# One broadcast multiply in place of eight scalings per row, and final waits in the order of the stores, in a grouped softmax

## The chip, the cores and the metric

One core of one Trainium2 chip. The metric is device time in microseconds (us), median of several executions; lower is better. A program on a single core gives "fast" runs here that lie within a few tenths of a microsecond, with a rare one 3 to 14 us above.

## The reference

```python
B, N, D, G = 4, 4096, 4352, 8          # x: float32
x_g = x.reshape(B, N, G, D // G)
x_g = x_g - x_g.max(axis=-1, keepdims=True)
exp = np.exp(x_g)
out = exp / exp.sum(axis=-1, keepdims=True)
```

A softmax over eight groups of 544 elements in each of 16384 rows. 285.2 MB are read and 285.2 MB written; the arithmetic is small.

## The kernel before

The 16384 rows are 64 tiles of 128 partitions by 2 rows (4.456 MB each). Six buffers in SBUF go round. SyncE issues the loads and, ahead of each after the sixth, waits for the store that frees the buffer. ScalarE issues the stores; the store of tile j-2 waits until VectorE has *seen* tile j land, so loads and stores alternate. VectorE takes the maxima of the next row before it scales the present one.

```python
P, R, NT, G, LAG = 128, 2, 6, 8, 2          # partitions, rows per tile, buffers, groups, lag of stores
def vector_max(n):
    s = n % S
    if s % R == 0:
        take(nc.vector, landed[s // R], 16)
        nc.vector.sem_inc(seen, 1)
    nc.vector.reduce_max(out=mx[:, s, :], in_=row(s), axis=X, negate=True).then_inc(max_done, 1)

def vector_scale(n):
    s = n % S
    take(nc.vector, exp_done)
    nc.vector.reciprocal(out=rs[:, s, :], in_=sm[:, s, :]).then_inc(rec_done, 1)
    take(nc.vector, rec_done)
    xr = row(s)
    for g in range(G):
        i = nc.vector.tensor_scalar_mul(
            out=xr[:, g, :], in0=xr[:, g, :], scalar1=rs[:, s, g:g + 1])
    i.then_inc(scaled, 1)
# ... scalar_exp: eight activations with accumulated sums; store: waits for `scaled`, R rows ...
for t in range(nt):
    b = t % NT
    if t >= NT:
        nc.sync.wait_ge(stored[b], 16 * (t // NT))
    nc.sync.dma_start(out=bufs[b][:, :], in_=xt[t]).then_inc(landed[b], 16)
for b in range(NT):
    nc.sync.wait_ge(stored[b], 16 * ((nt - b + NT - 1) // NT))
# ... VectorE: rows in the order vector_max(n + 1), vector_scale(n) ...
```

## Time and profile before

| | before |
|---|---|
| time, median of 3 | 1330.06 us (1329.78 to 1330.08) |
| span of the profiled execution | 1328.5 us |
| busy: VectorE, ScalarE | 78%, 58% |
| transfers | 570.4 MB, 429 GB/s over the span |
| last load landed, as seen by VectorE | 1280.54 us |
| last store issued | 1303.55 us |

How to read it: an engine that is busy 78% on average could still set the time in some stage, so ask in each stage who waits for whom. From 165 us on VectorE waits for a landing in each tile, and the DMA row is full; the transfers set the time.

### The profile page before, as it was taken

The numbers are of one execution on the slowest core, as the hardware profiler recorded it, in microseconds if no ns is written. First come the engines' busy times: TensorE is split into PE (matmuls) and PEld (weight loads), VectorE is DVE, ScalarE is ACT, GpSimd is POOL, SyncE is SP. The second block draws the span as 40 slices with busy tenths as digits, with TensorE's granted clock in tenths as the row PEclk, the third lists the DMA queues.
The fourth block names the chain that finished last, engine by engine and source line by source line (L and its number), as shares of the span: only waits on it lengthen the run. The fifth ranks groups of instructions, "written<-read, shape, count | busy, mean of one in ns | idle before, by whom it ended". The sixth has DMA issues, their size and how long they took to land. (4 is left out here: it accounts for less than half of the span.)

```text
span 1328.5 us, 4328 instructions
## 1 busy us (share of the span) xinstructions
DVE 1041.7 (78%) x1280; ACT 764.5 (58%) x2049; POOL 0.2 (0%) x4
## 2 busy tenths in 40 slices
DVE  5899987887877878778787787877878778787781
ACT  3677755655556556565565655655556555565551
POOL 0000000000000000000000000000000000000000
DMA  9999999999999999999999999999999999999997
GB/s 403 418 436 435 434 433 429 432 435 436 435 433 428 432 435 436 435 434 430 429 436 435 435 434 433 426 436 436 434 434 433 427 435 436 435 434 433 427 433 328
DMA packets 18439, 570.49 MB, mean 429 GB/s; under 512 B 2048, under 2 KB 2048, under 8 KB 2048
## 3 DMA queue, kind: packets, MB, share of 16 engines
q1 hardware_dynamic: 9216, 285.22, 49.8%
q10 hardware_dynamic: 9216, 285.22, 49.7%
q14 instruction: 7, 0.06, 0.0%
HBM read 285.21 MB, written 285.21 MB: 429 GB/s over the span
## 5 line engine op out<-in xcount | busy, mean ns | idle before, releaser
L88 ACT ACTIVATE xt<-xt,mx 128x544 f32<-128x544 f32 x1024 | 751.3, 735 | 534.1 <-ACTq L59 534.1
L70 DVE TENSOR_REDUCE mx<-xt 128x8 f32<-128x4352 f32 x128 | 599.2, 4682 | 238.3 <-DVEq L59 235.3
L79 DVE TENSOR_SCALAR xt<-xt,rs 128x544 f32<-128x544 f32 x1024 | 434.2, 498 | 19.2
L88 ACT ACTIVATION_READ_ACCUMULATOR xt<-xt,mx 128x1 f32 x1024 | 192.0, 187 | 0.0
L75 DVE RECIPROCAL rs<-sm 128x8 f32<-128x8 f32 x128 | 24.8, 193 | 4.2 <-DVEq L59 4.2
L120 ACT ACT_TABLE_LOAD x1 | 1.3, 1283 | 0.9 <-SPq L47 0.9
L156 POOL MEMSET const-bfloat16-1.0<- 128x1 bf16 x1 | 0.1, 103 | 0.0
L156 POOL MEMSET const-uint8-127<- 128x1 uint8 x1 | 0.1, 102 | 0.0
L156 POOL MEMSET const-float32-0.0<- 128x1 f32 x1 | 0.1, 100 | 0.2 <-issue 0.2
L156 POOL MEMSET const-float32-1.0<- 128x1 f32 x1 | 0.1, 99 | 0.0
## 6 DMA issues: line engine op xcount, KB each, us to landing
xt<-in_x_dram SPq DMA_DIRECT2D x64, 4352.0 KB, 30.5
out_dram<-xt ACTq DMA_DIRECT2D x64, 4352.0 KB, 51.3
```

What stands on the lines that cost most here:

```text
L70: nc.vector.reduce_max(out=mx[:, s, :], in_=row(s), axis=X, negate=True).then_inc(max_done, 1)
L75: nc.vector.reciprocal(out=rs[:, s, :], in_=sm[:, s, :]).then_inc(rec_done, 1)
L79: i = nc.vector.tensor_scalar_mul(out=xr[:, g, :], in0=xr[:, g, :], scalar1=rs[:, s, g:g + 1])
L88: i = nc.scalar.activation(out=xr[:, g, :], in_=xr[:, g, :], func=Exp, bias=mx[:, s, g:g + 1], scale=1.0, accum_out=sm[:, s, g:g + 1],)
L120: nc.scalar.preload_act_table(Exp)
L156: nc = _bacc.Bacc("TRN2", target_bir_lowering=False, num_devices=1)
```

## The change

The intent is to spend fewer VectorE instructions per row: one multiply of 4352 elements, whose second input repeats each group's reciprocal 544 times (a step of 0), in place of eight scalings of 544 elements. The final waits are put in the order in which the stores were issued. The "two rings" of its description, loads on one queue and stores on another, are in both kernels.

```diff
-        for g in range(G):
-            i = nc.vector.tensor_scalar_mul(
-                out=xr[:, g, :], in0=xr[:, g, :], scalar1=rs[:, s, g:g + 1])
-        i.then_inc(scaled, 1)
+        nc.vector.tensor_tensor(
+            out=xr,
+            in0=xr,
+            in1=rs[:, s, :].unsqueeze(2).to_broadcast([P, G, Dg]),
+            op=mybir.AluOpType.mult,
+        ).then_inc(scaled, 1)
...
-    for b in range(NT):
-        nc.sync.wait_ge(stored[b], 16 * ((nt - b + NT - 1) // NT))
+    for t in range(nt - NT, nt):
+        nc.sync.wait_ge(stored[t % NT], 16 * (t // NT + 1))
```

## The prediction

> **What bounds the kernel now.** I read the page first: the busy shares, the slices of DMA, the groups by line. Then the engines' waits, VectorE's timeline in the middle and at both ends, and the DMA share in short windows at the end.
>
> ```profile
> span 1328.5 us, 4328 instructions
> DVE 1041.7 (78%) x1280; ACT 764.5 (58%) x2049; POOL 0.2 (0%) x4
> DMA  9999999999999999999999999999999999999997
> HBM read 285.21 MB, written 285.21 MB: 429 GB/s over the span
> L70 DVE TENSOR_REDUCE mx<-xt 128x8 f32<-128x4352 f32 x128 | 599.2, 4682 | 238.3 <-DVEq L59 235.3
> L79 DVE TENSOR_SCALAR xt<-xt,rs 128x544 f32<-128x544 f32 x1024 | 434.2, 498 | 19.2
> L75 DVE RECIPROCAL rs<-sm 128x8 f32<-128x8 f32 x128 | 24.8, 193 | 4.2 <-DVEq L59 4.2
> ```
>
> No compute engine is full: VectorE (DVE) is busy 78% of the span, ScalarE 58%. The DMA row is full from the first slice to the last but one, at 429 GB/s. Each byte is moved once in and once out, 570.4 MB, so 128 tile moves of 4.456 MB. VectorE stands 235.3 us before its max reductions, and the releaser is a wait of its own queue: a tile that has yet to land. The timeline of VectorE in the middle shows one tile of two rows:
>
> ```profile
> 1239.18 4.68 DVE L70 TENSOR_REDUCE mx<-xt 128x8 f32<-128x4352 f32 x1 [4.09 <-DVEq L59]
> 1243.79 0.19 DVE L75 RECIPROCAL rs<-sm 128x8 f32<-128x8 f32 x1
> 1244.13 3.39 DVE L79 TENSOR_SCALAR xt<-xt,rs 128x544 f32<-128x544 f32 x8
> 1247.44 4.68 DVE L70 TENSOR_REDUCE mx<-xt 128x8 f32<-128x4352 f32 x1
> 1252.03 0.19 DVE L75 RECIPROCAL rs<-sm 128x8 f32<-128x8 f32 x1
> 1252.37 3.39 DVE L79 TENSOR_SCALAR xt<-xt,rs 128x544 f32<-128x544 f32 x8
> 1259.88 4.69 DVE L70 TENSOR_REDUCE mx<-xt 128x8 f32<-128x4352 f32 x1 [4.11 <-DVEq L59]
> ```
>
> A tile takes 1259.88 - 1239.18 = 20.70 us. VectorE works about 16.6 us of it and waits 4.1 us, and this wait returns every 20.7 us from 165 us on. At 20.7 us for two moves of 4.456 MB the DMA does 431 GB/s. So the steady stage is set by the transfers; VectorE has 4.1 us per tile, 2.05 us per row, to spare. The end, in windows (width, then busy of DVE, ACT, POOL, clock, DMA share, GB/s):
>
> ```profile
> 1280.60:1303.60 23.00, 19.82 (x29) 11.92 (x32) 0.00 (x0) 1.00 1.01 434
> 1303.60:1320.00 16.40, 0.00 (x0) 0.00 (x0) 0.00 (x0) 1.00 0.96 416
> 1320.00:1326.00 6.00, 0.00 (x0) 0.00 (x0) 0.00 (x0) 1.00 0.08 35
> ```
>
> The last store is issued at 1303.55, but a tile takes only 4.456 MB / 434 GB/s = 10.3 us and the DMA is full until about 1320. So 1320 - 1303.55 - 10.3 = about 6 us of older stores were still queued before it. Even the last store did not find idle transfer engines.
>
> **What the Trainium skill says.** "VectorE: DVE Perf Modes", section "The perf-mode tier table", gives fp32 tensor_scalar two elements per cycle and fp32 tensor_tensor and tensor_reduce one. The trace agrees for the kernel before: eight scalings of 544 take 3.39 us, fewer than 4352 / 0.96 GHz = 4.53 us, and the reduction takes 4.68 us. The same page, section "The TRN2 errata", gives (N+151)/0.96 GHz for an fp32 tensor_tensor: an estimate of 4503 / 0.96 = 4690 ns here, close to the 4682 ns that the one-per-cycle reduction over the same 4352 elements is measured at. No tensor_tensor is in this trace, so that part is not yet shown. "DMA: Bandwidth & Descriptors", section "Where 436 GB/s comes from", gives a ceiling of 435.2 GB/s at the SBUF ports. 429 over the span and 434 near the end agree: the floor is 570.4 MB / 435.2 = 1311 us, and the rest of the span is the first 2 us, the tail, and less than 1% of loss. The same section names some 358 GB/s for HBM as the bound; this trace shows more, and the measurement decides.
>
> **The change, part by part.** (1) It removes 1024 scalings of 544 elements; eight take 3.39 us, 3.31 us from their start to the next reduction's. The 498 ns mean counts overlap, so I don't multiply it by eight. (2) It adds 128 multiplies of 4352 elements at one element per cycle. I take 4.69 us each, 4.61 us to the next start (as between the reduction at 1239.18 and the reciprocal at 1243.79). So the change makes VectorE slower by 4.61 - 3.31 = 1.30 us per row, although it has 896 fewer instructions. VectorE's busy time becomes 599.2 + 24.8 + 128 x 4.69 = 1224 us, 92% of the span. A tile takes it 16.6 + 2.6 = 19.2 us, still under 20.7: the wait for a landing shrinks from 4.1 to about 1.5 us. Steady cost on the path: 0.
>
> (3) The start. Until about 165 us VectorE, not the DMA, is behind: it works without waiting for a landing and stores go out every 16.5 us. The first loads keep the DMA busy anyhow: six tiles x 10.3 us lasts to about 63 us. Store 0 is issued at 48.61 after two rows' scalings in the chain, so about 2.6 us later now. The next should be issued between 63 and 71 us, and later ones every 19.1 us. Store 0 and the last load share the DMA until about 73 us, so store 1 arrives just in time; from there a store every 19.1 us is faster than the 20.7 us that a load and a store take, and the DMA's queue only grows. Catching up takes far longer than before, up to some 500 us, since only 1.5 us is gained per tile. That is hidden, but the queue is thin from 60 to 100 us. I allow 0 to 3 us, most likely 0.5.
>
> (4) The end. From the last landing (1280.54) VectorE has three scalings to do. The last row's chain is: reduction of the last row after one slower scaling (+1.3), exponentials, then its own scaling (+1.3). So the last store is issued at 1303.55 + 2.6 = 1306.2. About 6 us were queued before it, so about 3.4 us still are. On average this is hidden; if some engines run dry early, up to 2.6 us show. I count 0.3.
>
> (5) The final waits. Loads go out on one queue and stores on another in both kernels; only the order of the six final waits changes. The wait for buffer 3 (the last store) is followed by two that are already met, at some 28 ns each in the trace: 0.06 us less. Nothing.
>
> Sum: 1330.06 + 0.5 + 0.3 - 0.06 = 1330.8 us.
>
> **The rivals.** (a) VectorE becomes the bound. It does if a row takes more than 20.7 / 2 = 10.35 us, thus if the multiply takes over 3.31 + 2.05 = 5.36 us to the next start. Against it: the reduction reads the same 4352 elements in 4.68 us. For it: two inputs, one of them a broadcast with step 0 inside, of which I have no measured line. At two cycles per element it would be about 9.1 us, a row 14 us, the whole 128 x 14 = about 1800 us. I give this 2%. A fixed cost of 0.7 us more per instruction would be needed for even the first loss. (b) The delays of the two ends show in full: 2.6 at the end and 3 at the start, 1335.7 us. For it: the queue is thin at the start, and at the end only 3.4 us of backlog is left. Against it: the DMA share near both points shows no hole, and it needs every store to miss. (c) Fewer and longer instructions speed things up: VectorE's sequencer is done with a row after one instruction instead of eight, so it signals a landing earlier in the catching-up stage, and the loop's first pass has less to fetch (3.05 us of idle at 56.38 now). It would help only where VectorE is late, in the first 165 us, and there the DMA is already full: no gain, at most 1 us.
>
> **Range and chances.** The time is set by 570 MB at the ceiling in both kernels, and three runs before lie within 0.3 us. So the range is the two ends: 1328.8 (small luck in the order of transfers) to 1334.5 (most of the delays of 3 and 2.6 us exposed). Two per cent is 26.6 us; only rival (a) gets there. Faster 0.01, same 0.95, slower 0.04.
>
> **What would show it right or wrong.** Right: line 79 or so has 128 TENSOR_TENSOR of about 4690 ns; VectorE at about 1224 us and 92%; waits before reductions fall from 235 us to under 80 us (fewer than 40 tiles x 1.5 us, plus the first 14); 20.7 us from landing to landing in the middle; about 429 GB/s; the last store issued about 2.6 us later and landing at the same time. Wrong: a multiply over 5.3 us, with no waits for landings left; or DMA slices under 9 between 60 and 120 us; or a tail in which the DMA share falls before the last store is issued.

## The result, and the profile after

| | before | after |
|---|---|---|
| time, median of 4 runs each | 1330.07 us (1329.78 to 1330.17) | 1329.45 us (1329.36 to 1332.93) |
| ratio of fast runs, 95% interval | | 1.0002 (0.9985 to 1.0019) |
| VectorE busy | 1041.7 us | 1206.9 us |
| last store issued | 1303.55 us | 1305.42 us |

The same time, while VectorE works 165 us more. Ratios here and below are the mean time of one kernel's fast runs over that of the other's in the same rounds, so not quite the ratio of the medians; the single run at 1332.93 lifts this one over 1.

The page of the kernel after, with the lines that answer to those of before (after the bar: busy us, mean ns of one; then idle us ahead of it and what ended it):

```profile
span 1327.6 us, 3432 instructions
DVE 1206.9 (91%) x384; ACT 764.3 (58%) x2049; POOL 0.2 (0%) x4
DMA  9999999999999999999999999999999999999997
HBM read 285.21 MB, written 285.21 MB: 430 GB/s over the span
L70 DVE TENSOR_REDUCE mx<-xt 128x8 f32<-128x4352 f32 x128 | 599.0, 4681 | 76.7 <-DVEq L59 75.2
L78 DVE TENSOR_TENSOR xt<-xt,rs 128x4352 f32<-128x4352 f32 x128 | 600.6, 4692 | 18.8
```

The multiply takes 4692 ns, the wait for landings fell from 235.3 to 75.2 us, and the DMA row has not changed. VectorE's timeline shows one tile late in the steady stage (lines of its second row left out):

```profile
1238.48 4.68 DVE L70 TENSOR_REDUCE mx<-xt 128x8 f32<-128x4352 f32 x1 [1.48 <-DVEq L59]
1243.08 0.19 DVE L75 RECIPROCAL rs<-sm 128x8 f32<-128x8 f32 x1
1243.42 4.69 DVE L78 TENSOR_TENSOR xt<-xt,rs 128x4352 f32<-128x4352 f32 x1
1248.03 4.68 DVE L70 TENSOR_REDUCE mx<-xt 128x8 f32<-128x4352 f32 x1
...
1259.16 4.68 DVE L70 TENSOR_REDUCE mx<-xt 128x8 f32<-128x4352 f32 x1 [1.50 <-DVEq L59]
```

A tile still takes 1259.16 - 1238.48 = 20.68 us. From reduction to reduction a row is 9.55 us; it was 8.26. The 2.6 us that a tile's two rows gained came out of the wait, 4.1 to 1.5 us. This wait first shows at 453 us, where before it showed at 165 us: that is how long VectorE took to catch up with the landings.

### The profile page after: what moved, and what is told of

Its sections match the earlier page's. It is cut to its first block, busy times and chain, and to the rows that moved or that the text cites. A ratio compares the mean times of both kernels' runs of the same rounds, so it can differ in the third digit from the quotient of the medians.

```text
span 1327.6 us, 3432 instructions
## 1 busy us (share of the span) xinstructions
DVE 1206.9 (91%) x384; ACT 764.3 (58%) x2049; POOL 0.2 (0%) x4
## 5 line engine op out<-in xcount | busy, mean ns | idle before, releaser
L70 DVE TENSOR_REDUCE mx<-xt 128x8 f32<-128x4352 f32 x128 | 599.0, 4681 | 76.7 <-DVEq L59 75.2
L78 DVE TENSOR_TENSOR xt<-xt,rs 128x4352 f32<-128x4352 f32 x128 | 600.6, 4692 | 18.8
```

What stands on the lines that cost most here:

```text
L78: nc.vector.tensor_tensor(out=xr, in0=xr, in1=rs[:, s, :].unsqueeze(2).to_broadcast([P, G, Dg]), op=mybir.AluOpType.mult,).then_inc(scaled, 1)
```

## The experiments

The chip that each set ran on also ran the kernel before in the same rounds; its medians are given beside.

### The kernels' spread, and the parts one by one

**The changed kernel again, twice** (no edit).

> The changed kernel unaltered, to see whether the 0.6 us between the medians (1329.45 after, 1330.07 before) and the one run at 1332.93 come back. Theory (transfers set the time, the change is hidden): within 1 us of before, both ways. Rival (the thinner transfer queue of the first 440 us costs now and then): more runs of this kernel than of before at 1332 or over.

Measured: 1329.51 us (1329.42 to 1329.99), before 1330.29 (1329.87 to 1330.82), ratio 0.9995 (0.9981 to 1.0009).

> The changed kernel unaltered beside them: 1329.4 to 1329.6 if the two earlier sets hold, about 0.7 us under before, with perhaps one run at 1333.

Measured: 1329.51 us (1329.44 to 1329.68), before 1330.21 (one run of before at 1344.47), ratio 0.9984 (0.9951 to 1.0018). So 0.6 to 0.8 us less in each of three sets, below what the intervals resolve. The run at 1332.93 did not come back in these eleven; a rare long run is nothing that only the changed kernel has.

**The final waits alone**: the second half of the diff applied to the kernel before.

> Kernel before with only the final waits reordered. Theory: two waits of 28 ns less, 0.06 us, so not to be told from before (within 0.3 us). Rival (the 0.6 us by which the changed kernel is faster comes from the waits): 0.5 us or more under before.

Measured: 1330.08 us (1329.93 to 1330.20), before 1330.29, ratio 0.9998 (0.9985 to 1.0012). Its range lies inside that of before. The waits are worth nothing that shows.

**Eight scalings at both ends**:

```diff
+        if n < LAG * R or n >= rest * R:
+            for g in range(G):
+                i = nc.vector.tensor_scalar_mul(
+                    out=xr[:, g, :], in0=xr[:, g, :], scalar1=rs[:, s, g:g + 1])
+            i.then_inc(scaled, 1)
+            return
         nc.vector.tensor_tensor(
```

> Changed kernel with the eight scalings put back in the four rows before the loop and the four after it, one multiply in the 120 rows between. Theory (both ends are hidden): same as the changed kernel within 0.5 us, although the last store is issued 2 to 3 us earlier. Rival (the delays at the ends show): 2 to 5 us faster than the changed kernel.

Measured: 1329.80 us (1329.35 to 1333.80), against 1329.51 for the changed kernel. In its trace the last store was issued at 1304.47, 1.3 us earlier than in the changed kernel's trace (1305.76), not 2 to 3 us, for its last tile landed 1.3 us later (the first reduction after it starts at 1281.47 against 1280.16); from landing to store it is the foretold 2 to 3 us less. No gain: what the two ends together lose on VectorE does not show in the time.

**A dense second input**, result wrong on purpose:

```diff
-            in1=rs[:, s, :].unsqueeze(2).to_broadcast([P, G, Dg]),
+            in1=xr,
```

> The multiply reads the row itself as second input in place of the broadcast reciprocals (result wrong on purpose: squares of the exponentials). Theory (one element per cycle whatever the second input is): 4690 ns each, same time. Rival (the stride of 0 makes the broadcast cheaper or dearer than a dense input): a duration that differs by over 50 ns; below 4600 or above 4740 ns.

Measured: 1329.53 us, and the group's line in its profile:

```profile
L78 DVE TENSOR_TENSOR xt<-xt 128x4352 f32<-128x4352 f32 x128 | 600.5, 4692 | 18.8
```

4692 ns again. The broadcast with a step of 0 costs and saves nothing against a dense input (here the same row, read twice).

### How much VectorE has to spare

Two doses of useless work on VectorE, ahead of each reciprocal; nobody reads the result (the line that allocates `junk` is left out here and below):

```diff
+        nc.vector.reduce_max(out=junk[:, s, :], in_=row(s)[:, :, :48], axis=X)    # small dose; :200 is the large
         nc.vector.reciprocal(out=rs[:, s, :], in_=sm[:, s, :]).then_inc(rec_done, 1)
```

> Changed kernel plus one reduction of 8x48 elements per row on VectorE, whose result nobody reads: an estimate of 0.48 us per row, 61 us in all. Changed kernel waits 1.49 us per tile for a landing, so 0.74 us per row are to spare. Theory (slack hides it): same time within 2 us, the wait per tile down to about 0.5 us, VectorE's busy share about 96%. Rival (any slowing of VectorE shows): 20 to 60 us slower.

Measured: 1329.06 us (1328.99 to 1329.18), before 1330.29, ratio 0.9991 (0.9976 to 1.0006).

> The same with 8x200 elements: an estimate of 1.74 us per row. A row is then 9.54 + 1.74 = 11.28 us against 10.33 us that the transfers take for it. Theory (VectorE becomes the bound past 0.74 us): 14 + 128 x 11.28 + about 5 of waits + 15 to 20 for the last store = 1478 to 1484 us, no waits for landings in the middle, DMA at about 395 GB/s. Rival (transfers still hide it): under 1340 us.

Measured: 1475.69 us (1475.55 to 1475.79), ratio 1.1092 (1.1075 to 1.1109). Two lines of the page and one of the waits of each (waits: us in total, times, longest), the small dose first:

```profile
DVE 1263.2 (95%) x512; ACT 765.2 (58%) x2049; POOL 0.2 (0%) x4
L76 DVE TENSOR_REDUCE junk<-xt 128x8 f32<-128x384 f32 x128 | 69.4, 543 | 2.5 <-DVEq L60 2.5
DVE mx L71 <- DVEq L60: 20.3, 12, 14.1
```

```profile
DVE 1424.2 (97%) x512; ACT 764.9 (52%) x2049; POOL 0.2 (0%) x4
L76 DVE TENSOR_REDUCE junk<-xt 128x8 f32<-128x1600 f32 x128 | 231.5, 1809 | 1.7 <-DVEq L60 1.7
DVE mx L71 <- DVEq L60: 14.1, 1, 14.1
```

The small dose adds 56 us to VectorE's busy time and nothing to the kernel: nearly all of it, 55 us, came out of waiting. In its timeline VectorE catches up with the landings only at 1073 us. With the large dose one wait is left, the one for the first tile, so VectorE is the bound; a row then takes 11.27 us in its timeline, and 128 of them are 1443 us of the 1474 us span. The sum of the expectation, 1478 to 1484 us, was 2 us too high. So the step of the prediction that matters most, that VectorE stays hidden while a row takes less than 10.35 us, holds with the bound on either side of it: 9.55 us (the change) and 10.01 us (the change with the small dose, in its timeline) are free, 11.27 us is not. Nothing between 10.01 and 11.27 us was tried.

### Why the end does not show

> Changed kernel with two whole-row reductions (9.2 us) on VectorE ahead of the last row's reciprocal, so the last store is issued about 9.2 us later, at 1314.6. Theory A (one of the 16 transfer engines is some 5 us behind the others at the end and alone sets it, and it still has work queued): 0 to 2 us slower than the changed kernel. Theory B (the 3.4 us of backlog that the prediction took from the mean rate): 5 to 6 us slower. Theory C (the last store finds idle engines): 9 us slower.

```diff
+        if n == nt * R - 1:
+            for k in range(2):
+                nc.vector.reduce_max(out=junk[:, k, :], in_=row(s), axis=X)
         nc.vector.reciprocal(out=rs[:, s, :], in_=sm[:, s, :]).then_inc(rec_done, 1)
```

Measured: 1329.85 us (1329.64 to 1329.91), before 1330.29 in the same rounds, ratio 0.9996 (0.9983 to 1.0010). The last store was issued at 1314.76, 9 us later than without the edit, and the time hardly moved: 0.3 to 0.4 us above the changed kernel in its other sets (1329.45 to 1329.51). The issue of the last store in the changed kernel, then in this one:

```profile
1305.42 0.34 ACTq L102 DMA_DIRECT2D out_dram<-xt  x1
1314.76 0.34 ACTq L106 DMA_DIRECT2D out_dram<-xt  x1
```

The end of both in windows (width, busy of DVE, ACT, POOL, clock, DMA share, GB/s), the changed kernel first, then this one:

```profile
1306.00:1310.00 4.00, 0.00 (x0) 0.00 (x0) 0.00 (x0) 1.00 1.01 435
1310.00:1315.00 5.00, 0.00 (x0) 0.00 (x0) 0.00 (x0) 1.00 1.00 432
1315.00:1320.00 5.00, 0.00 (x0) 0.00 (x0) 0.00 (x0) 1.00 0.89 383
1320.00:1322.00 2.00, 0.00 (x0) 0.00 (x0) 0.00 (x0) 1.00 0.12 52
1322.00:1326.00 4.00, 0.00 (x0) 0.00 (x0) 0.00 (x0) 1.00 0.04 17
```

```profile
1306.00:1310.00 4.00, 3.85 (x3) 0.00 (x0) 0.00 (x0) 1.00 0.81 348
1310.00:1315.00 5.00, 4.65 (x1) 0.00 (x0) 0.00 (x0) 1.00 0.08 35
1315.00:1320.00 5.00, 0.00 (x0) 0.00 (x0) 0.00 (x0) 1.00 1.04 446
1320.00:1322.00 2.00, 0.00 (x0) 0.00 (x0) 0.00 (x0) 1.00 0.65 279
1322.00:1326.00 4.00, 0.00 (x0) 0.00 (x0) 0.00 (x0) 1.00 0.97 418
```

In the delayed kernel the transfer engines stand nearly idle from 1310 to 1315: the mean backlog is used up. Yet the end is the same. The 0.04 in the changed kernel's last line says why: 0.04 of 16 engines is less than one engine. The trace also holds the moment at which each of the 16 engines reported its part of a transfer, though not which engine it was. For the last store, from the median engine to the last one:

| kernel | median engine to last engine |
|---|---|
| before | 6.4 us |
| after | 5.6 us |
| last store 9 us later | 0.1 us |

One engine of sixteen falls behind in the course of the run and ends it alone. Among the loads the last report lies 0.3 to 0.4 us behind the median at 102 us, before and after; 3 us by about 640 us before and 760 us after; and 6.2 and 5.5 us for the last load. The distance to the last report but one grows with it, so from about 500 us on it is a single engine. In the changed kernel the other fifteen have reported by 1322.7 us and the late one at 1326.0, so a store that comes 9 us late costs the fifteen their lead. The late engine loses almost nothing: in the delayed kernel's trace its last move of the store before ends at 1315.39 us and the first moves of the delayed store start at 1315.60, so it stood for 0.2 us. A delay much over 9 us should then show; none was tried. Theory A stands, and B and C fall.

**Relief for the late engine.** If that engine were the sixteenth, a last store over 120 rows and then 8 rows should spare it:

```diff
-        nc.sync.wait_ge(stored[t % NT], 16 * (t // NT + 1))
+        nc.sync.wait_ge(stored[t % NT], 16 * (t // NT + 1 + (t == nt - 1)))
...
-    store((nt - 1) % NT, ot[nt - 1])
+    b = (nt - 1) % NT
+    take(nc.scalar, scaled, R)
+    nc.scalar.dma_start(out=ot[nt - 1][:120], in_=bufs[b][:120, :]).then_inc(stored[b], 16)
+    nc.scalar.dma_start(out=ot[nt - 1][120:], in_=bufs[b][120:, :]).then_inc(stored[b], 16)
```

> Changed kernel with the last tile's store cut into 120 rows (over 15 transfer engines) and 8 rows (over 8), so the sixteenth engine has nothing of it. Theory A (that engine is the straggler that ends the kernel): 3.5 to 4.5 us faster than the changed kernel. Theory A with another engine as straggler: the same, or 1.3 us slower. Theory B (the engines end together): about 1 us slower, since 8 engines get a ninth row.

Measured: 1339.88 us (1339.82 to 1339.90), ratio 1.0072 (1.0058 to 1.0086): 10 us slower, which no theory had. Its end in windows:

```profile
1310.00:1318.00 8.00, 0.00 (x0) 0.00 (x0) 0.00 (x0) 1.00 0.89 248
1318.00:1326.00 8.00, 0.00 (x0) 0.00 (x0) 0.00 (x0) 1.00 0.83 226
1326.00:1336.00 10.00, 0.00 (x0) 0.00 (x0) 0.00 (x0) 1.00 0.12 45
```

The engines are 0.8 to 0.9 busy but move little more than half of the usual 432 GB/s, so the cut itself made the moves slow. The Trainium skill ("DMA: Bandwidth & Descriptors", section "Why a DMA increments its semaphore by 16 and not by 1") says that a transfer of this kind uses the largest number of engines up to 16 that divides the outer dimension. The trace agrees: 23 reports (15 and 8) came late, between 1320 and 1337 us, and two at once, within 0.7 us of the issues, for what is missing to 16 and 16. It also shows where the time went: moving one row took an engine 1.29 us (the median, in this run as in the others), but 68 of the 140 moves that start after 1308.5 us took more than 1.6 us and up to 5.2 us, where the changed kernel has none over 1.3 us. It shows no reason for that, and the run does not tell which engine is late. Both stay open. No faster version came of it.

### Where the 0.7 us are

All kernels with the multiply, but for the large dose and the cut store, came out a little under before. A kernel with the eight scalings and the old waits, but a dose (8x147 elements) that makes VectorE about as slow as after, asks whether the slower VectorE is the reason:

```diff
+        nc.vector.reduce_max(out=junk[:, s, :], in_=row(s)[:, :, :147], axis=X)
         nc.vector.reciprocal(out=rs[:, s, :], in_=sm[:, s, :]).then_inc(rec_done, 1)
```

> Kernel before (eight scalings, old final waits) plus a reduction of 8x147 elements per row on VectorE, an estimate of 1.26 us per row from the 0.44 and 1.70 us that the two doses added: VectorE as slow as in the changed kernel, with more instructions instead of fewer. All kernels with a slower VectorE have come out 0.4 to 1.2 us under before. Theory 1 (a slower VectorE, thus fewer moves queued in the first 440 us, makes the transfers a little better): 0.5 to 1 us under before, and the last landing at about 1279.8. Theory 2 (fewer instructions fetched in the loop): not under before. Theory 3 (chance of the layout of runs): no order.

Measured: 1330.08 us (1329.82 to 1330.23), before 1330.21, ratio 0.9988 (0.9954 to 1.0021). Its lines:

```profile
DVE 1204.8 (91%) x1408; ACT 764.8 (58%) x2049; POOL 0.2 (0%) x4
DVE mx L71 <- DVEq L60: 74.9, 42, 14.1
```

VectorE was busy 1204.8 us, as after (1206.9), and waited 74.9 us for landings, as after (75.2), but the time is that of before. Theory 1 falls.

> The small dose again, on the chip and in the rounds of the two others. Theory 1: 0.3 to 0.6 us under the changed kernel again. Theory 2: as the changed kernel. Theory 3: anything within 1 us.

Measured: 1328.68 us (1328.38 to 1329.19); the changed kernel beside it 1329.51. Below the changed kernel again, by 0.8 us, with more instructions than it, so theory 2 does not cover this either. (Alone, this run would have fitted theory 1.) For the last store the late engine lies 4.9 us behind the median in this kernel's trace, 5.6 after, 6.4 before, while the median engines agree within 0.3 us. The other traces whose end was left alone fall in the same order: 6.3 us with the final waits alone and 6.1 us in the run above, both with the eight scalings and at the time of before; 5.7 to 5.8 us in the two repeats and with the dense input, at the time of after; 5.2 us in the first run of the small dose. (With eight scalings at both ends it is 5.2 us too, but there the median engine itself ends 0.7 us later than after.) So the differences of 0.7 and 0.8 us lie in how far one engine falls behind. Why that depends on the kernel is not settled.

## Why the prediction was right

- **The bound.** Transfers at 429 to 430 GB/s before and after, a tile in 20.7 us. The doses show it from both sides.
- **The multiply's cost.** 4690 ns predicted, 4692 measured; 1.30 us more per row predicted, 9.55 - 8.26 = 1.29 measured. Only the sum of busy times, 1224 us, was too high by 17 us: it adds durations that overlap by about 0.08 us at each junction, as the prediction itself warned for the 498 ns.
- **The start.** Store 0 was to come 2.6 us later and came 1.25 us later (49.86 against 48.61): before, it stood about 1 us after the exponentials ahead of it had ended, and after it came at once. Store 1 came at 66.93, in the foretold 63 to 71; the following ones every 19.1 us. The DMA's slices show no hole that before has not: in windows of 10 us the two lowest rates from 40 to 140 us are 388 and 404 GB/s after, 388 and 400 before, in the same windows. The 0.5 us allowed for it did not show. VectorE caught up at 453 us ("up to some 500").
- **The end.** The last store came 1305.42 - 1303.55 = 1.9 us later, not 2.6; counted from the last landing, which came 0.7 us earlier, it is the 2.6. (A landing, too, ends with the late engine: before, the last report of the last load came at 1280.31 us and the reduction started at 1280.54; after, 1279.59 and 1279.82.) The verdict, hidden, was right, but its reason fell short: not 3.4 us of mean backlog, but a whole engine that is 6 us late and takes up the store only 10 us after it is issued (1315.76 against 1305.42). The line with a DMA share of 0.08 after 1320 was shown in the prediction and not read as one engine.
- **The rivals.** VectorE as the bound needed 10.35 us per row and was seen only with the large dose. The ends in full (1335.7) did not show. Rival (c) had its 3.05 us of idle fall to 1.51, worth nothing.
- **The sum.** 1330.8 predicted, 1329.45 measured: the 0.8 us for the ends were not there, and 0.6 us came off at the late engine, which the prediction did not have. The lower end of its range, "small luck in the order of transfers", covered that without its cause; this part was luck, the bound and the slack were not.

## What to carry to other kernels

Fewer instructions are not less work: eight fp32 scalings took 3.39 us per row, the one multiply 4.69 us, and only a wait for transfers hid the 165 us. Count the slack of the engine off the path per tile (here 4.1 us, of which the change spent 2.6), since a later change finds only the rest. At the end of a transfer-bound kernel ask whether all transfer engines end together: a share of 0.04 of 16 engines, less than one, hints at a straggler, and work ahead of the last store is free as long as the straggler hides it.

## What the Trainium skill lacked or had wrong

- "DMA: Bandwidth & Descriptors", section "Where 436 GB/s comes from": it names about 358 GB/s from HBM as the bound of transfers between HBM and SBUF, beside a measurement of its own of 425 GB/s; these runs hold 429 to 430 GB/s over the whole span.
- "DMA: Bandwidth & Descriptors", section "Latency and other measured facts": it says that engines 7 and 15 are usually slower, with a best guess at a cause that only transfers issued from GpSimd have. Here one engine fell behind by 5 to 6 us in 1320 us with transfers issued from SyncE and ScalarE; which one these runs do not tell.
- "DMA: Bandwidth & Descriptors", section "Why a DMA increments its semaphore by 16 and not by 1": nothing is said of the rate of a store over 15 engines; with the last store cut into 120 and 8 rows the transfers fell to 248 and 226 GB/s.
- "Vector Engine (DVE) Microarchitecture Reference", section "Performance modes — why throughput varies by op and dtype": for a step of 0 in a two-source operation it lists operands of 2 bytes; with fp32 the multiply took 4692 ns, as with a dense second input.
